# Scores of a differential attention: four products over 128 rows for a component and block of queries, or six over 64 rows

## The chip, the cores and the metric

The kernel runs on one core of one Trainium2 chip. Its time is the device time of one launch in microseconds (us); the kernel before took 3059.82 us (median of 3 runs, 3057.39 to 3063.07). The work is spread over the core's engines, which run side by side and meet at semaphores: TensorE (PE for its products, PEld for the loads of the stationary operand), VectorE (DVE), ScalarE (ACT), GpSimd (POOL), and SyncE (SP), which issues the DMAs.

## The reference, cut to what matters

The program is a two-layer block followed by a second, one-layer block. Each layer of the first block has three branches; the change touches one of them, the differential attention with 4 heads, each with two components of 64 channels, over 1024 positions:

```
def diff_branch(q, k, v, g, ..., pos):
    q = q.reshape(b_, l_, DIFF_HEADS, 2, DIFF_HD).transpose(3, 0, 2, 1, 4)
    k = k.reshape(b_, l_, DIFF_HEADS, 2, DIFF_HD).transpose(3, 0, 2, 1, 4)
    q = rope(q, pos) * (DIFF_HD ** -0.5)
    k = rope(k, pos)
    ...
    def block(qblk):                       # 128 queries at a time
        s = jnp.einsum('cbhqd,cbhkd->cbhqk', qblk, k).astype(jnp.float32)
        p = jax.nn.softmax(s, axis=-1)
        w = p[0] - lam * p[1]
        return jnp.einsum('bhqk,bhkv->bhqv', w.astype(v.dtype), v)
```

So for each of 2 layers, 4 heads and 8 blocks of 128 queries, two score matrices of 128 x 1024 are needed, one for each component, each a product over 64 channels. All data are float32.

## The kernel before, in words

**Products in two parts.** Float32 values that go through the large products are split into a high part H (rounded to the type fp32r) and a low part L = value - H, both of which are stored as fp32r. A product of two such values is taken as H\*H + H\*L + L\*H. `split` does the splitting: a copy on ScalarE (L162) and a subtraction on VectorE (L163).

**Preparing a head.** `diff_prep` projects queries and keys of one head (128 channels, two components of 64), 512 positions at a time, applies the rotary embedding (`raw`, a copy `xs` with channel groups swapped by four DMAs, two products on GpSimd, a sum on VectorE) and then stacks: for component 0 the tile `q0` holds H in its rows 0 to 63 and L in rows 64 to 127, for component 1 `q1` holds L above and H below; the same for `k0` and `k1`. That takes two half-height copies on ScalarE (L773, L774) and two half-height subtractions on VectorE (L775, L776) for each 512 positions. For the keys, two more tiles `ksw` are made by four DMAs (L781, L782), with the halves of `k0` and `k1` swapped. All are tiles of the tag "in" (10 buffers in common with other work); `raw` and `xs` share the two buffers of the tag "pr".

**Scores.** `diff_attend` then needs, for a component and 512 keys, two products over all 128 rows: stack times stack (L797: H\*H + L\*L) and stack times swapped stack (L798: H\*L + L\*H). For a block of 128 queries that makes 2 components x 2 halves of the keys x 2 = 8 products with 512 columns. A component's 1024 scores lie in a PSUM tile `psc` of the tag "big", of which there are two. VectorE takes the negative maximum (L800), ScalarE the exponential with its sum (L803), which also ends the use of the `psc` tile. The weights are combined on VectorE and GpSimd, transposed on TensorE (`pt`, L822), copied (`wT`, L823), and multiplied with the values (`pav`, L827).

**What sets the order.** The program is written as generators: while a head's blocks run, a `Filler` puts projections of later heads (`pj`, L234) between them, so many microseconds' worth per step (RATE); for the last head the output projection (`output`, `pout`, L724) takes that place. A scheduler orders the instructions of each engine from that: at each point it takes, of those whose operands and buffers it reckons to be ready, the one of highest priority. Each engine then works through its list strictly in order, and waits at semaphores. `Burst` is a helper of other stages of the kernel (L388, L411, L452): its first product has the priority of its place, and all later ones of the burst have a much higher one and are tied behind the first. It does not ask that they all be ready when the first is. Products there use part of the rows of the array: `psl` (L411) has 32 or 64 rows to a product, each row group writing a PSUM bank of its own.

The stages that matter here: attention of layer 1 runs from about 432 to 822 us (heads 0 to 3 start at about 432, 540, 638 and 709 us), of layer 2 from about 1281 to 1667 us (1281, 1397, 1484, 1555). From 754 and 1600 us on the output projection runs beside the last head.

Of the kernel before, what the change touches and what calls it, by code (L numbers as in the profile page):

```python
# [9 lines left out]
F32 = mybir.dt.float32  # L10
F32R = mybir.dt.float32r
U8 = mybir.dt.uint8
AF = mybir.ActivationFunctionType
ALU = mybir.AluOpType
# [4 lines left out]
P = 128  # L19
T = 1024  # L20
# [138 lines left out]
def split(k, raw, H, L, leng=None):  # L159

    nc = k.nc
    nc.scalar.copy(H, raw)  # L162
    (leng or nc.vector).tensor_tensor(L, raw, H.bitcast(F32), ALU.subtract)  # L163
# [88 lines left out]
def proj_cm(k, W, c0, m, half):  # L252

    ps = k.pj.tile([P, 512], F32, tag="pj", name="pj")
    terms = []
    for kt in range(KT):
        wh, wl = W.part(kt)
        hh, hl = k.hH[half][:, kt, :], k.hL[half][:, kt, :]
        terms += [(x[:, c0:c0 + m], y) for x, y in ((wh, hh), (wh, hl), (wl, hh))]
    yield from accumulate(k, ps[:m, :], terms)  # L260
    return ps
# [16 lines left out]
def rstd_of(k, ssq, n, scale, pool, tag):  # L278

    nc = k.nc  # L280
    r = pool.tile([P, n], F32, tag=tag, name=tag)
    nc.gpsimd.tensor_scalar(r, ssq, scale, EPS, ALU.mult, ALU.add)  # L282
    nc.gpsimd.tensor_tensor(r, r, k.mhalf[:, :n], ALU.pow)  # L283
    return r
# [216 lines left out]
def layer(k, l, xin, xout):  # L501
# [110 lines left out]
    for pair in range(2):  # L612
        F.add(f"d{2 * pair}", diff_prep(k, 2 * pair, w_in))
        F.add(f"dv{pair}", values(1824 + pair * 256, ("at", "v")[pair]))
        F.add(f"dg{pair}", gates(2336 + pair * 256, slice(128, 256)))
        F.add(f"d{2 * pair + 1}", diff_prep(k, 2 * pair + 1, w_in))
# [39 lines left out]
    for hd in range(4):  # L656
        stk = F.need(f"d{hd}")
        v, sg = F.need(f"dv{hd // 2}"), F.need(f"dg{hd // 2}")
        att = diff_attend(k, l, hd, stk, v, (hd % 2) * P, sg)
        if hd < 3:  # L660
            run(beside(att, mods), RATE["diff"][hd])
            continue
        for _ in mods:
            pass
        if l == DEPTH - 1:
            for _ in context_norm(k):
                pass
        F.drain()
        out = output(k, l, xin, xout)
        next(out)  # L670
        for i, _ in enumerate(att):
            if i > 2 and i % 3 == 2:
                next(out)
        early = context(k) if l == DEPTH - 1 else iter(())
        for _ in out:
            pass
        k.tc.cur_priority -= EARLY
        for _ in early:
            pass
        k.tc.cur_priority += EARLY  # L680
# [71 lines left out]
def diff_prep(k, hd, w_in):  # L752

    nc = k.nc
    Wq = Weights(k, w_in[:, 800 + hd * P:928 + hd * P], P)
    Wk = Weights(k, w_in[:, 1312 + hd * P:1440 + hd * P], P)
    stk = {}
    for nm, W in (("q", Wq), ("k", Wk)):
        s0 = k.wk.tile([P, T], F32R, tag="in", name=nm + "0")
        s1 = k.wk.tile([P, T], F32R, tag="in", name=nm + "1")  # L760
        for half in range(2):
            hs = slice(half * 512, half * 512 + 512)
            ps = yield from proj_cm(k, W, 0, P, half)
            raw = k.wk.tile([P, 512], F32, tag="pr", name="raw")
            xs = k.wk.tile([P, 512], F32, tag="pr", name="xs")
            nc.scalar.activation(raw, ps, AF.Copy, scale=0.125 if nm == "q" else 1.0)  # L766
            for g in range(4):
                g2 = g ^ 1
                nc.sync.dma_start(xs[g * 32:g * 32 + 32, :], raw[g2 * 32:g2 * 32 + 32, :])
            nc.gpsimd.tensor_tensor(raw, raw, k.rcos[:, hs], ALU.mult)  # L770
            nc.gpsimd.tensor_tensor(xs, xs, k.rsin[:, hs], ALU.mult)
            nc.vector.tensor_tensor(raw, raw, xs, ALU.add)
            nc.scalar.copy(s0[0:64, hs], raw[0:64, :])  # L773
            nc.scalar.copy(s1[64:128, hs], raw[64:128, :])  # L774
            nc.vector.tensor_tensor(s0[64:128, hs], raw[0:64, :], s0[0:64, hs].bitcast(F32), ALU.subtract)  # L775
            nc.vector.tensor_tensor(s1[0:64, hs], raw[64:128, :], s1[64:128, hs].bitcast(F32), ALU.subtract)  # L776
        stk[nm] = (s0, s1)
    sw = []
    for c in range(2):
        s = k.wk.tile([P, T], F32R, tag="in", name="ksw")  # L780
        nc.sync.dma_start(s[0:64, :].bitcast(F32), stk["k"][c][64:128, :].bitcast(F32))  # L781
        nc.sync.dma_start(s[64:128, :].bitcast(F32), stk["k"][c][0:64, :].bitcast(F32))  # L782
        sw.append(s)
    return stk["q"], stk["k"], sw


def diff_attend(k, l, hd, stks, v, vc0, sg):
    nc = k.nc
    sq_, sk, sw = stks
    for qt in range(NT):  # L790
        qs = slice(qt * P, qt * P + P)
        ps_, Z = [], []
        for c in range(2):
            ps = k.big.tile([P, T], F32, tag="big", name="psc")
            for kh in range(2):
                ks = slice(kh * 512, kh * 512 + 512)
                nc.tensor.matmul(ps[:, ks], sq_[c][:, qs], sk[c][:, ks], start=True, stop=False)  # L797
                k.mark = nc.tensor.matmul(ps[:, ks], sq_[c][:, qs], sw[c][:, ks], start=False, stop=True)  # L798
            nm = k.st.tile([P, 1], F32, tag="nm", name="nm")
            nc.vector.tensor_reduce(nm, ps, axis=AX.X, op=ALU.max, negate=True)  # L800
            p = k.wk.tile([P, T], F32, tag="U" if c and qt % 2 and hd < 3 else "be", name="p")
            z = k.st.tile([P, 1], F32, tag="Z", name="Z")
            nc.scalar.activation(p, ps, AF.Exp, bias=nm, accum_out=z)  # L803
            ps_.append(p)
            Z.append(z)
        rz = k.st.tile([P, 2], F32, tag="rz", name="rz")
        nc.vector.reciprocal(rz[:, 0:1], Z[0])
        nc.vector.reciprocal(rz[:, 1:2], Z[1])
        sc = k.st.tile([P, 1], F32, tag="sc", name="sc")
        nc.vector.scalar_tensor_tensor(sc, Z[0], rz[:, 1:2], k.nlam[:, l:l + 1], ALU.mult, ALU.mult)  # L810
        yield
        w = ps_[0]
        a, b = slice(0, W_CUT), slice(W_CUT, T)
        nc.vector.scalar_tensor_tensor(w[:, a], ps_[1][:, a], sc, ps_[0][:, a], ALU.mult, ALU.add)
        nc.gpsimd.tensor_scalar_mul(ps_[1][:, b], ps_[1][:, b], sc)  # L815
        nc.gpsimd.tensor_tensor(w[:, b], ps_[1][:, b], ps_[0][:, b], ALU.add)
        wT = k.wk.tile([P, KT, P], F32, tag="at", name="wT")
        for g in range(2):
            pt = k.sm.tile([P, 512], F32, tag="sm", name="pt")
            for j in range(4):  # L820
                c = g * 4 + j
                k.mark = nc.tensor.transpose(pt[:, j * P:(j + 1) * P], w[:, c * P:(c + 1) * P], k.ident)  # L822
            nc.scalar.copy(wT[:, g * 4:g * 4 + 4, :], pt.rearrange("p (j t) -> p j t", j=4))  # L823
        yield
        po = k.sm.tile([P, 512], F32, tag="sm", name="pav")
        for kt in range(KT):
            k.mark = nc.tensor.matmul(po[:, :P], wT[:, kt, :], v[kt][:, vc0:vc0 + P], start=kt == 0, stop=kt == KT - 1)  # L827
        sq = k.st.tile([P, 256], F32, tag="sq", name="sq", bufs=1)
        ss = k.st.tile([P, 1], F32, tag="ss", name="ss")
        nc.scalar.activation(sq[:, :P], po[:, :P], AF.Square, scale=rz[:, 0:1], accum_out=ss)  # L830
        r = rstd_of(k, ss, 1, 1.0 / P, k.st, "rs")
        rr = k.st.tile([P, 1], F32, tag="rr", name="rr")
        nc.vector.tensor_tensor(rr, r, rz[:, 0:1], ALU.mult)
        y = k.wk.tile([P, 256], F32, tag="y", name="y")
        nc.vector.scalar_tensor_tensor(y[:, :P], po[:, :P], rr, sg[qt][:, vc0:vc0 + P], ALU.mult, ALU.mult)
        nc.sync.dma_start(k.ydram[qt][:, 256 + hd * P:384 + hd * P], y[:, :P])
        yield
# [585 lines left out]
HEADS = (slice(0, 64), slice(64, 128))  # L1423
# [635 lines left out]
```

## Time and profile before

| what | before |
|---|---|
| median of 3 runs | 3059.82 us |
| the profiled execution, its own time | 3056.68 us |
| span of its instructions | 3054.9 us |
| TensorE products busy | 2770.3 us (91%) |
| VectorE busy | 1881.9 us (62%) |
| ScalarE busy | 1251.4 us (41%) |
| GpSimd busy | 1010.8 us (33%) |
| mean granted clock of TensorE | 0.962 of full |

The profiled execution took 1.8 us more than its span; that stretch lies outside the instructions. Busy time of TensorE is made of modelled ends: a product of 512 columns is shown as 0.40 us long, while the next starts 0.23 us after it. What a product costs the engine is therefore read from the starts of neighbours (called the pitch below), and not from the durations.

### The profile page before, as it was taken

To read this page: it belongs to the slowest core of one execution; us is meant where nothing else is said; L and a number is where in the kernel's file an instruction comes from. 1 tells how busy PE (TensorE), PEld (TensorE's weight loads), DVE (VectorE), ACT (ScalarE), POOL (GpSimd) and SP (SyncE) were. 2 spreads that over 40 slices of the span, in tenths; PEclk is the share of its full clock that TensorE was granted. 3 is DMA by queue.
4 is the path that set the end of the run, shared out by engine and by line. 5 is a ranking of instruction groups with operands and counts; after the bars stand their busy time and mean duration, and the time that the engine had idled before them with its cause. 6 is when DMAs were issued, how large, how long until landed. Compare 5 with 4: busy or idle time off the path is not lost. (4 is left out here: it accounts for less than half of the span.)

```text
span 3054.9 us, 56014 instructions
## 1 busy us (share of the span) xinstructions
PE 2770.3 (91%) x21790; PEld 2344.4 (77%) x21790; DVE 1881.9 (62%) x3777; ACT 1251.4 (41%) x2791; POOL 1010.8 (33%) x1124
## 2 busy tenths in 40 slices
PE   7899889897989998899979899998888999989999
PEld 4788677885768887788958778886776677769889
DVE  4668686566445686866564456576777664346661
ACT  4222145655434212355554443434353433345520
POOL 1224447754202243476452123321332120010042
PEclk9899899998999998999989999998999999999999
DMA  3111122324331101223243535352445361254463
GB/s 112 29 44 36 39 66 77 90 54 132 114 140 32 43 29 38 67 83 93 69 126 120 172 92 144 108 143 75 110 124 129 94 167 47 61 161 134 152 205 97
DMA packets 353346, 294.02 MB, mean 96 GB/s; under 512 B 145174, under 2 KB 302742, under 8 KB 353080
## 3 DMA queue, kind: packets, MB, share of 16 engines
q1 hardware_dynamic: 353080, 290.43, 32.7%
q8 instruction: 172, 2.82, 0.4%
q14 instruction: 94, 0.77, 0.1%
HBM read 198.79 MB, written 74.78 MB: 90 GB/s over the span
## 5 line engine op out<-in xcount | busy, mean ns | idle before, releaser
L163 DVE TENSOR_TENSOR wL<-wr,wH 128x512 fp32r<-128x512 f32 (+1 forms) x259 | 200.0, 776 | 244.8 <-ACT wH L162 235.3
L234 PE MATMUL pj<-wH,hH 128*128 128x256 f32 x1024 | 295.3, 290 | 16.7 <-ACT wH L162 10.7
L234 PE MATMUL pj<-wL,hH 128*128 128x256 f32 x1024 | 292.8, 286 | 2.4 <-DVE wL L163 2.4
L234 PE MATMUL pj<-wH,hL 128*128 128x256 f32 x1024 | 291.8, 285 | 0.0
L162 ACT CAST wH<-wr 128x512 fp32r<-128x512 f32 (+1 forms) x259 | 159.1, 617 | 297.3 <-PE pj L234 181.2
L234 PE MATMUL pj<-H,wH 128*128 128x512 f32 (+1 forms) x592 | 242.4, 412 | 5.6 <-DVE naz L1608 4.1
L234 PE MATMUL pj<-H,wL 128*128 128x512 f32 (+1 forms) x592 | 243.6, 412 | 0.0
L234 PE MATMUL pj<-L,wH 128*128 128x512 f32 (+1 forms) x592 | 242.7, 410 | 0.0
L234 PE MATMUL pj<-hH,wH 128*128 128x512 f32 (+1 forms) x544 | 222.6, 410 | 11.9 <-ACT raw L766 7.3
L234 PE MATMUL pj<-hL,wH 128*128 128x512 f32 (+1 forms) x544 | 223.2, 410 | 0.0
L234 PE MATMUL pj<-hH,wL 128*128 128x512 f32 (+1 forms) x544 | 222.6, 409 | 0.6 <-DVE wL L163 0.6
L234 PEld LDWEIGHTS pj<-wH,hH 128*128 128x128 f32 x1024 | 194.8, 191 | 24.2 <-ACT wH L162 12.0
L282 POOL TENSOR_SCALAR rs<-ss 128x1 f32<-128x1 f32 (+2 forms) x190 | 62.9, 331 | 442.1 <-DVE ss L730 135.2
L234 PEld LDWEIGHTS pj<-wL,hH 128*128 128x128 f32 x1024 | 195.3, 191 | 6.5 <-DVE wL L163 3.7
L234 PEld LDWEIGHTS pj<-wH,hL 128*128 128x128 f32 x1024 | 195.2, 191 | 2.3
L800 DVE TENSOR_REDUCE nm<-psc 128x1 f32<-128x1024 f32 x128 | 155.0, 1217 | 35.2 <-PE psc L798 34.9
L803 ACT ACTIVATE p<-psc,nm 128x1024 f32<-128x1024 f32 x128 | 142.9, 1117 | 75.5 <-DVE nm L800 45.4
L827 PE MATMUL pav<-v,wT 128*128 128x128 f32 x1024 | 138.4, 286 | 17.7 <-ACT wT L823 15.7
L827 PEld LDWEIGHTS pav<-v,wT 128*128 128x128 f32 x1024 | 130.2, 200 | 30.8 <-ACT wT L823 24.9
L283 POOL TENSOR_TENSOR rs<-rs,mhalf 128x1 f32<-128x1 f32 (+2 forms) x190 | 148.0, 782 | 11.6
L815 POOL TENSOR_SCALAR p<-p,sc 128x320 f32<-128x320 f32 x64 | 102.6, 1603 | 126.3 <-DVE sc L810 92.7
L234 PEld LDWEIGHTS pj<-H,wH 128*128 128x128 f32 (+1 forms) x592 | 112.1, 189 | 31.9 <-DVE naz L1608 4.5
(426 smaller groups left out, 7692.5 us busy)
## 6 DMA issues: line engine op xcount, KB each, us to landing
wr<-in_w_in_dram SPq DMA_DIRECT2D x240, 256.0 KB
modw<-in_mod_w_dram SPq DMA_DIRECT2D x48, 256.0 KB
xs<-raw SPq DMA_DIRECT2D x128, 64.0 KB
ksw<-k SPq DMA_DIRECT2D x32, 256.0 KB
wor<-in_w_out_dram SPq DMA_DIRECT2D x16, 512.0 KB
yt<-y SPq DMA_DIRECT2D x16, 512.0 KB
xh<-xh SPq DMA_DIRECT2D x32, 256.0 KB
gd<-gth SPq DMA_DIRECT2D x32, 256.0 KB
```

The costliest lines, as they stand in the source:

```text
L162: nc.scalar.copy(H, raw)
L163: (leng or nc.vector).tensor_tensor(L, raw, H.bitcast(F32), ALU.subtract)
L234: mm = k.nc.tensor.matmul(ps, x, y, start=i == 0, stop=i == len(terms) - 1)
L282: nc.gpsimd.tensor_scalar(r, ssq, scale, EPS, ALU.mult, ALU.add)
L283: nc.gpsimd.tensor_tensor(r, r, k.mhalf[:, :n], ALU.pow)
L800: nc.vector.tensor_reduce(nm, ps, axis=AX.X, op=ALU.max, negate=True)
L803: nc.scalar.activation(p, ps, AF.Exp, bias=nm, accum_out=z)
L815: nc.gpsimd.tensor_scalar_mul(ps_[1][:, b], ps_[1][:, b], sc)
L827: k.mark = nc.tensor.matmul(po[:, :P], wT[:, kt, :], v[kt][:, vc0:vc0 + P], start=kt == 0, stop=kt == KT - 1)
```

## The change

Queries and keys are now split as whole tiles of 128 rows: `H` and `L` of `q`, `H` and `L` of `k`, with component 0 in rows 0 to 63 and component 1 in rows 64 to 127, by one `split` for each 512 positions. The swapped tiles and their DMAs are gone. For a block of queries, both `psc` tiles are taken first, and twelve products in a `Burst` follow: for each half of the keys and each of H\*H, H\*L and L\*H, one product over rows 0 to 63 (component 0) and one over rows 64 to 127 (component 1), in turn. L\*L is no longer computed. `HEADS` are these two row slices.

```diff
--- before.py
+++ after.py
@@ -756,8 +756,8 @@
     Wk = Weights(k, w_in[:, 1312 + hd * P:1440 + hd * P], P)
     stk = {}
     for nm, W in (("q", Wq), ("k", Wk)):
-        s0 = k.wk.tile([P, T], F32R, tag="in", name=nm + "0")
-        s1 = k.wk.tile([P, T], F32R, tag="in", name=nm + "1")
+        H = k.wk.tile([P, T], F32R, tag="in", name=nm + "H")
+        L = k.wk.tile([P, T], F32R, tag="in", name=nm + "L")
         for half in range(2):
             hs = slice(half * 512, half * 512 + 512)
             ps = yield from proj_cm(k, W, 0, P, half)
@@ -770,32 +770,25 @@
             nc.gpsimd.tensor_tensor(raw, raw, k.rcos[:, hs], ALU.mult)
             nc.gpsimd.tensor_tensor(xs, xs, k.rsin[:, hs], ALU.mult)
             nc.vector.tensor_tensor(raw, raw, xs, ALU.add)
-            nc.scalar.copy(s0[0:64, hs], raw[0:64, :])
-            nc.scalar.copy(s1[64:128, hs], raw[64:128, :])
-            nc.vector.tensor_tensor(s0[64:128, hs], raw[0:64, :], s0[0:64, hs].bitcast(F32), ALU.subtract)
-            nc.vector.tensor_tensor(s1[0:64, hs], raw[64:128, :], s1[64:128, hs].bitcast(F32), ALU.subtract)
-        stk[nm] = (s0, s1)
-    sw = []
-    for c in range(2):
-        s = k.wk.tile([P, T], F32R, tag="in", name="ksw")
-        nc.sync.dma_start(s[0:64, :].bitcast(F32), stk["k"][c][64:128, :].bitcast(F32))
-        nc.sync.dma_start(s[64:128, :].bitcast(F32), stk["k"][c][0:64, :].bitcast(F32))
-        sw.append(s)
-    return stk["q"], stk["k"], sw
+            split(k, raw, H[:, hs], L[:, hs])
+        stk[nm] = (H, L)
+    return stk["q"], stk["k"]
 
 
 def diff_attend(k, l, hd, stks, v, vc0, sg):
     nc = k.nc
-    sq_, sk, sw = stks
+    (qH, qL), (kH, kL) = stks
     for qt in range(NT):
         qs = slice(qt * P, qt * P + P)
         ps_, Z = [], []
-        for c in range(2):
-            ps = k.big.tile([P, T], F32, tag="big", name="psc")
+        pss = [k.big.tile([P, T], F32, tag="big", name="psc") for _ in range(2)]
+        with Burst(k) as burst:
             for kh in range(2):
                 ks = slice(kh * 512, kh * 512 + 512)
-                nc.tensor.matmul(ps[:, ks], sq_[c][:, qs], sk[c][:, ks], start=True, stop=False)
-                k.mark = nc.tensor.matmul(ps[:, ks], sq_[c][:, qs], sw[c][:, ks], start=False, stop=True)
+                for i, (x, y) in enumerate(((qH, kH), (qH, kL), (qL, kH))):
+                    for c, r in enumerate(HEADS):
+                        burst(nc.tensor.matmul(pss[c][:, ks], x[r, qs], y[r, ks], start=i == 0, stop=i == 2))
+        for c, ps in enumerate(pss):
             nm = k.st.tile([P, 1], F32, tag="nm", name="nm")
             nc.vector.tensor_reduce(nm, ps, axis=AX.X, op=ALU.max, negate=True)
             p = k.wk.tile([P, T], F32, tag="U" if c and qt % 2 and hd < 3 else "be", name="p")
```

The scheduler's list for TensorE shows where the products stand. `k0`, `q0`, `k1`, `q1` and `ksw` are the old tiles, `kH`, `kL`, `qH` and `qL` the new ones; two numbers behind `psc` are the two components of one block of queries. Before, at the first block of head 0 in layer 1:

```order
L234 MATMUL pj_3940<-wH_3924,hH_184 128x256 [waits Activation_49]
L797 MATMUL psc_4464<-k0_3345,q0_3082 128x512
L798 MATMUL psc_4464<-ksw_3532,q0_3082 128x512
L797 MATMUL psc_4474<-k1_3346,q1_3083 128x512
L234 MATMUL pj_3940<-wL_3925,hH_184 128x256 [waits DVE_49]
L234 MATMUL pj_3940<-wH_3924,hL_186 128x256
L234 MATMUL pj_3940<-wH_3924,hH_184 128x256
L234 MATMUL pj_3940<-wL_3925,hH_184 128x256
L234 MATMUL pj_3940<-wH_3924,hL_186 128x256
L798 MATMUL psc_4474<-ksw_3535,q1_3083 128x512 [waits DMAHW1_49,DMAHW0_49]
L797 MATMUL psc_4474<-k1_3346,q1_3083 128x512
```

After, at the same block:

```order
L234 MATMUL pj_3926<-wH_3904,hH_184 128x256 [waits Activation_49]
L790 MATMUL psc_4450<-kH_3341,qH_3082 128x512
L790 MATMUL psc_4451<-kH_3341,qH_3082 128x512
L790 MATMUL psc_4450<-kL_3342,qH_3082 128x512
L790 MATMUL psc_4451<-kL_3342,qH_3082 128x512
L790 MATMUL psc_4450<-kH_3341,qL_3083 128x512
L790 MATMUL psc_4451<-kH_3341,qL_3083 128x512
L790 MATMUL psc_4450<-kH_3341,qH_3082 128x512
L790 MATMUL psc_4451<-kH_3341,qH_3082 128x512
```

Here the two components stand in turn, twelve products in one piece, and the projection `pj` that stood between the parts of the second component has moved behind them. Before, at the second block of head 2 in layer 1, the first component (its second component stands some 25 rows later, behind other products):

```order
L234 MATMUL pj_6309<-wH_5807,hL_187 128x256
L797 MATMUL psc_6778<-k0_5111,q0_4925 128x512 [waits Activation_49]
L798 MATMUL psc_6778<-ksw_5293,q0_4925 128x512
L797 MATMUL psc_6778<-k0_5111,q0_4925 128x512
L798 MATMUL psc_6778<-ksw_5293,q0_4925 128x512
L822 MATMUL pt_6554<-ident_60,p_6518 128x128 [waits Activation_49]
L822 MATMUL pt_6554<-ident_60,p_6518 128x128 [waits Pool_49]
```

After, at the same block:

```order
L234 MATMUL pj_6391<-wH_5789,hL_187 128x256
L790 MATMUL psc_6800<-kH_5099,qH_4909 128x512 [waits Activation_49]
L790 MATMUL psc_6800<-kL_5100,qH_4909 128x512
L790 MATMUL psc_6800<-kH_5099,qL_4910 128x512
L790 MATMUL psc_6800<-kH_5099,qH_4909 128x512
L790 MATMUL psc_6800<-kL_5100,qH_4909 128x512
L790 MATMUL psc_6800<-kH_5099,qL_4910 128x512
L820 MATMUL pav_6599<-v_3725,wT_6565 128x128 [waits Activation_49]
L820 MATMUL pav_6599<-v_3725,wT_6565 128x128 x3
L815 MATMUL pt_6664<-ident_60,p_6639 128x128 [waits PE_49]
L790 MATMUL psc_6801<-kH_5099,qH_4909 128x512 [waits Activation_49]
L790 MATMUL psc_6801<-kL_5100,qH_4909 128x512
```

Here the six products of one component stand in a row, all over the same 64 rows, then other products over 128 rows, and then the six of the other component, which have a wait of their own for ScalarE. Counted over all 64 blocks (2 layers x 4 heads x 8), the new list has the 768 products in 93 unbroken groups; 163 pairs of them stand in turn as written (326 products), and 442 products stand behind one of the same component or of another block. By layer and head:

| layer, head | pairs | products alone | groups |
|---|---|---|---|
| 1, 0 | 36 | 24 | 10 |
| 1, 1 | 32 | 32 | 9 |
| 1, 2 | 6 | 84 | 15 |
| 1, 3 | 2 | 92 | 14 |
| 2, 0 | 36 | 24 | 10 |
| 2, 1 | 30 | 36 | 11 |
| 2, 2 | 13 | 70 | 13 |
| 2, 3 | 8 | 80 | 11 |

The other stages that use parts of the rows (L388, L411, L452) keep their number of groups.

## Rows read from the trace of the kernel before

**Rows 1.** The page's first part: busy us, share of the span and instructions by engine.

```profile
PE 2770.3 (91%) x21790; PEld 2344.4 (77%) x21790; DVE 1881.9 (62%) x3777; ACT 1251.4 (41%) x2791; POOL 1010.8 (33%) x1124
```

**Rows 2.** Busy time by stretch of the differential attention, both layers.

```profile
core 0: us, PE busy (x) PEld busy (x) DVE busy (x) ACT busy (x) POOL busy (x), PEclk, DMA share, GB/s
432.00:540.00 108.00, 100.41 (x618) 86.89 (x618) 76.31 (x133) 63.90 (x142) 78.24 (x78) 1.00 0.32 88
...
638.00:709.00 71.00, 67.41 (x416) 58.02 (x415) 47.31 (x82) 41.53 (x87) 40.97 (x43) 1.00 0.22 56
709.00:754.00 45.00, 29.52 (x137) 23.45 (x136) 30.46 (x53) 24.52 (x50) 17.75 (x20) 0.78 0.55 156
...
1484.00:1555.00 71.00, 67.08 (x413) 57.72 (x412) 46.91 (x80) 41.10 (x84) 39.79 (x40) 1.00 0.21 54
1555.00:1600.00 45.00, 26.96 (x136) 21.83 (x135) 30.81 (x55) 25.43 (x54) 25.38 (x30) 0.81 0.57 173
...
sum 776.00, PE 703.00 PEld 606.58 DVE 488.46 ACT 437.13 POOL 429.94; mean PE 70.30 PEld 60.66 DVE 48.85 ACT 43.71 POOL 42.99
```

**Rows 3.** Waits of TensorE, 432 to 822 us: us in all, times, longest.

```profile
PE pj L234 <- ACT raw L766: 8.0, 5, 3.4
PE pt L822 <- DVE y L835: 8.0, 4, 5.2
...
PE psc L798 <- DMA ksw<-k: 3.2, 1, 3.2
```

**Rows 4.** The same, 1281 to 1667 us.

```profile
PE psc L797 <- ACT p L803: 10.6, 9, 3.2
...
PE pj L234 <- ACT raw L766: 2.9, 3, 1.8
...
PE psc L798 <- DMA ksw<-k: 0.6, 1, 0.6
```

**Rows 5.** Groups of the score products: shapes, count | busy us, mean ns | idle before.

```profile
L797 PE MATMUL psc<-k,q 128*128 128x512 f32 x256 | 109.1, 427 | 16.2 <-ACT p L803 16.2
...
L798 PE MATMUL psc<-ksw,q 128*128 128x512 f32 x256 | 104.4, 408 | 3.7 <-DMA ksw<-k 3.7
```

**Rows 6.** TensorE in order of time in head 2: start us, us long, what.

```profile
658.52 0.40 PE L797 MATMUL psc<-k,q 128*128 128x512 f32 x1
658.75 0.39 PE L798 MATMUL psc<-ksw,q 128*128 128x512 f32 x1
658.98 0.39 PE L797 MATMUL psc<-k,q 128*128 128x512 f32 x1
```

**Rows 7.** TensorE in order of time around a burst of 64-row products.

```profile
1140.13 0.28 PE L234 MATMUL pj<-wL,hH 128*128 128x256 f32 x1
1140.35 1.16 PE L411 MATMUL psl<-Qt,Kt 64*128 64x128 f32 x16
1141.44 0.39 PE L234 MATMUL pj<-wH,hL 128*128 128x256 f32 x1
1141.66 0.28 PE L234 MATMUL pj<-wH,hH 128*128 128x256 f32 x1
1141.78 0.28 PE L234 MATMUL pj<-wL,hH 128*128 128x256 f32 x1
```

**Rows 8.** TensorE in order of time around a burst of 32-row products.

```profile
119.21 1.17 PE L411 MATMUL psl<-Qt,Kt 32*128 32x128 f32 x32
120.32 0.38 PE L234 MATMUL pj<-wH,hH 128*128 128x256 f32 x1
```

**Rows 9.** Stacking the keys: ns min/median/max, first and last start, forms.

```profile
L773 ACT CAST k<-raw x16: 602/618/621, 402.1 to 1557.9; 64x512 fp32r<-64x512 f32 x16
...
L775 DVE TENSOR_TENSOR k<-raw,k x16: 684/794/1523, 405.1 to 1559.4; 64x512 fp32r<-64x512 f32 x16
```

**Rows 10.** TensorE in order of time in head 3, at the second swapped tile.

```profile
726.37 0.50 PE L798 MATMUL psc<-ksw,q 128*128 128x512 f32 x1 [3.15 <-DMA ksw<-k]
```

## The prediction

> **What bounds the kernel now.** I read the page first: TensorE is busy 91% of the span, the next engine 62% [rows 1]. That is an average, so the stretches of the differential attention come next [rows 2]. The reader is to see that in head 2 TensorE is busy 67.4 of 71 us in layer 1 and 67.1 of 71 in layer 2, with VectorE and ScalarE at two thirds or less: there every product that is added in its list pushes the rest back. The opening of head 3 is another matter (709 to 754 and 1555 to 1600 us): TensorE is busy 29.5 and 27.0 of 45 us, at a mean granted clock of 0.78 and 0.81, so part of these stretches runs at the lower of the two levels, 1.2 GHz; a chain of other work sets the pace. Over all ten stretches TensorE is idle 776.0 - 703.0 = 73.0 us. The waits say for what: for `raw`, which frees the PSUM buffer of a projection, 8.0 + 2.9 us; for `ksw`, 3.2 + 0.6 us; the rest for steps of the softmax [rows 3, 4].
>
> **The score products.** Before, there are 512, all over 128 rows [rows 5]. Busy time misleads, since ends are modelled; the starts of neighbours stand 0.23 us apart (658.52, 658.75, 658.98) [rows 6]; that pitch is what a product costs. 512 x 0.23 = 117.8 us of TensorE.
>
> After, there are 768 over 64 rows. What a pair costs is not in the trace for 512 columns, so I take it from narrower ones. A burst of 16 products over 64 rows, two row groups in turn, starts at 1140.35 and lasts 1.16 us; a burst of 32 over 32 rows, four row groups in turn, lasts 1.17 [rows 7, 8]. Eight rounds either way: with four products to a round the time is that of two, so row groups in turn run side by side. For a pair of 512 columns the bounds are thus 0.23 (side by side) and 0.46 (one after the other); I take 0.23, the case that the rows show. Two products behind one another over the same row group don't share anything: they cost 0.23 each, as products over 128 rows do, for the columns are the same 512.
>
> Such a burst also costs something at its edges. From the last `pj` ahead of it (1140.13) to the second behind it (1141.66) are 1.53 us; two `pj` pitches of 0.12 (1141.66 to 1141.78) and eight rounds of 0.11 leave 1.53 - 0.23 - 0.89 = 0.40 us [rows 7]. It lies at the front, where the array empties and the first weights are loaded with nothing beside them, and again at the back (1141.44 to 1141.66 is 0.22 where 0.12 is usual). The other burst is as long from its start to the next `pj`, 1.11 us against 1.09 [rows 7, 8]. Bounds for the edges of a burst of 512-column products: 0, if wide products hide them, and 0.40; I take 0.40, since emptying and a first load don't depend on the columns that follow.
>
> Now the list of TensorE. Written as pairs, all 64 blocks would need 6 x 0.23 + 0.40 = 1.78 us against 8 x 0.23 = 1.84: little is to be had, 4 us in all. But the list has only 163 pairs; 442 products stand alone and there are 93 groups. The reason is visible in its waits: the two `psc` buffers come free one after the other, each at the end of an exponential; the first product of the burst needs only component 0, it is placed as soon as that buffer is reckoned free, and the five others of component 0, with the highest priority of all, follow at once while component 1 is not ready. A block split so costs 12 x 0.23 + 2 x 0.40 = 3.56 us, 1.72 more than before. The sum: (163 + 442) x 0.23 + 93 x 0.40 = 139.2 + 37.2 = 176.4 us, less 117.8: **+58.6 us** of TensorE, of which by the table of pairs and groups heads 0 and 1 bring 14.6 and heads 2 and 3 bring 44.0. A burst that stays whole must also wait for both exponentials, with TensorE's whole list behind it; a wait for one costs 1.2 us today (10.6 us in 9) [rows 4]. Since such a burst stays whole only where both buffers are reckoned free, I take 0; the most is one such wait for each of the 25 whole blocks, 30 us.
>
> **What it removes.** For each 512 positions of q or k two ScalarE copies of 0.62 us become one over 128 rows, and two VectorE subtractions of 0.69 (the lesser ends; one median is 0.79) become one [rows 9]. These engines are not the bound, so this counts only where TensorE waits for `raw`: `raw` and `xs` share two buffers, so the next `raw` waits until the last subtraction has read the old one, and that chain is 1.3 us shorter. TensorE waits for it 5 + 3 times, 10.9 us; 8 x 1.3 = 10.4 is the most, 0 the least; I take -7. The `ksw` DMAs (8 MB over the program) go with their waits, 3.8 us on TensorE, the longest at 726.37 [rows 10]; where such a wait goes, the softmax of the same blocks is next and not far behind. I take -4 (0 to -8, as VectorE too starts earlier there).
>
> **What is covered.** In the two openings of head 3 there is idle TensorE time, 15.5 and 18.0 us [rows 2]; three to four split blocks fall in each, 6 us a layer. These added products also lie on the chain of their blocks, so I let half be covered, -6 (0 to -12). Of the other 73.0 - 33.5 = 39.5 us of idle time some waits are for a step that started after a score product and are not shortened; I let -5 (0 to -12) go. If the cover is gone, both terms are zero.
>
> Sum: 58.6 - 7 - 4 - 6 - 5 = **+37 us**. On the profiled execution, 3056.7 + 37 = 3094; that one lies 3.1 us under the median of the runs, so for the median I forecast 3097. Its own range: with nothing gained and nothing covered 3118; with edges half as large and every gain at its most 58.6 - 18.6 - 10.4 - 8 - 12 - 12 = -2, so 3058. Neither end is likely with all its terms together; I keep 3070 to 3122.
>
> **A rule weighed.** In the trace, weight loads run behind products over the same rows: `pj` products of 256 columns stand 0.12 apart although each brings its own load, and a load with nothing beside it showed as 0.10 more (0.22 against 0.12) [rows 7]. In the Trainium skill, "TensorE: Matmul & The Clock Gate", section "Part 3: Packing small matmuls", a load overlaps products in flight only when its row group differs. Here the trace disagrees for full height, and in the burst too, where in each round of 0.11 both row groups take a new load; by the rule the products that stand alone would each pay for theirs.
>
> **Rivals.** (a) The waits take it: the idle 73.0 us swallow the added 58.6, and the removed waits show. Place: all heads; price: all covered, 10.9 + 3.8 gained, 3045. It decides when more than 44 of the 58.6 fall into idle time. Against it: head 2 alone gains 12.0 and 9.6 us of products where TensorE is idle 3.6 and 3.9. (b) No gain and no loss: the edges cost nothing with wide products (-37) and the cover is as I have it: 58.6 - 37.2 - 22 = -1, 3059. For it: no burst of 512 columns is in the trace. Against: the 0.40 is the same for 16 and 32 products. (c) The pairs don't run side by side at 512 columns, the change doesn't do what it says: 163 x 0.23 = +37 more, so 3134. Against it: the two bursts [rows 7, 8]. (d) Loads over the same row group are not hidden: 442 x 0.10 = +44 more, so 3141; the trace speaks against it, as said.
>
> **How the numbers follow.** Forecast 0.80; (a) 0.07, (b) 0.05, (c) 0.05, (d) 0.03. A difference of 0.2%, 6 us, is about what a measurement here can tell from none. Faster comes from (a): 0.07. Within 0.2% comes from (b) and 0.01 of the forecast's lower tail: 0.06. Slower is the rest of the forecast with (c) and (d): 0.87. The range for 8 in 10: the forecast's own, 3070 to 3122, holds nearly all of its 0.80; stretched to 3066 below and 3124 above.
>
> **What would show it.** In the profile after, a pair of `psc` products should start within 0.01 us of each other and the next pair 0.23 later; products alone should stand 0.23 apart; each group should lose about 0.4 us at its edges. Head 2 should be longer by about 10 us in each layer, heads 0 and 1 by a few us together, the opening of head 3 by little or nothing; the waits for `ksw` must be gone, and those for `raw` less. VectorE and ScalarE should lose some 22 and 20 us of busy time. I am wrong if head 2 keeps its length, if a group shows no edges, or if the time that heads 0 and 1 gain by a shorter preparation outweighs their 14.6.

## The result and the profile after

| | before | after |
|---|---|---|
| median, 4 runs each | 3058.67 us (3057.39 to 3063.07) | 3105.43 us (3096.87 to 3107.78) |
| profiled execution, own time | 3056.7 us | 3105.35 us |
| its span | 3054.9 us | 3103.6 us |
| TensorE busy in it | 2770.3 us | 2828.8 us |

The ratio is 1.0145, with a 95% interval of 1.0123 to 1.0167: the change makes the kernel slower by 47 us. The forecast was 3097 us, range 3066 to 3124.

The page's first part of the kernel after, the line that answers to [rows 1]:

```profile
PE 2828.8 (91%) x22046; PEld 2370.6 (76%) x22046; DVE 1841.1 (59%) x3745; ACT 1230.3 (40%) x2759; POOL 1003.6 (32%) x1124
```

TensorE has 58.5 us more, in 256 more products; VectorE has 40.8 less and ScalarE 21.1 less.

Next, TensorE of the kernel after in order of time (start us, us long, what), first around a group that stayed whole, then around a block that was split. An "x2" row is two products at practically the same start, one of each component:

```profile
489.86 0.40 PE L234 MATMUL pj<-hH,wL 128*128 128x512 f32 x1
490.18 0.50 PE L790 MATMUL psc<-kH,qH 64*128 64x512 f32 x2
490.52 0.39 PE L790 MATMUL psc<-kL,qH 64*128 64x512 f32 x2
490.75 0.40 PE L790 MATMUL psc<-kH,qL 64*128 64x512 f32 x2
490.99 0.39 PE L790 MATMUL psc<-kH,qH 64*128 64x512 f32 x2
491.22 0.40 PE L790 MATMUL psc<-kL,qH 64*128 64x512 f32 x2
491.45 0.40 PE L790 MATMUL psc<-kH,qL 64*128 64x512 f32 x2
491.78 0.66 PE L815 MATMUL pt<-ident,p 128*128 128x128 f32 x4
...
654.68 0.49 PE L790 MATMUL psc<-kH,qH 64*128 64x512 f32 x1
655.02 0.39 PE L790 MATMUL psc<-kL,qH 64*128 64x512 f32 x1
655.25 0.39 PE L790 MATMUL psc<-kH,qL 64*128 64x512 f32 x1
655.48 0.39 PE L790 MATMUL psc<-kH,qH 64*128 64x512 f32 x1
655.71 0.39 PE L790 MATMUL psc<-kL,qH 64*128 64x512 f32 x1
655.93 0.39 PE L790 MATMUL psc<-kH,qL 64*128 64x512 f32 x1
656.25 1.16 PE L820 MATMUL pav<-v,wT 128*128 128x128 f32 x8
```

Read the distances of the starts. Six pairs take 1.27 us from the first start to the last and 1.60 to the next TensorE work; six products alone take 1.25 and 1.57. So a pair costs what one product costs, and a product alone does half the work in the same time. The usual distance is 0.23. The excess stands at the edges: 0.32 instead of 0.23 ahead of the first group (489.86 to 490.18), 0.34 to its second pair, 0.33 behind its last. A fourth piece follows behind the first product over 128 rows after a group, as in [rows 7], where 0.22 stood in place of 0.12. Four pieces of about 0.1 make the 0.40 of the forecast.

The waits of TensorE after, for the two stretches of [rows 3] and [rows 4], 400 to 870 us and 1281 to 1720 us (us in all, times, longest):

```profile
PE psc L790 <- ACT p L796: 11.1, 5, 5.4
PE pav L820 <- DVE y L828: 6.0, 3, 2.7
PE pt L815 <- DVE y L828: 5.0, 3, 3.7
...
PE pj L234 <- ACT raw L766: 0.4, 1, 0.4
```

```profile
PE pav L820 <- DVE y L828: 8.7, 6, 2.5
PE psc L790 <- ACT p L796: 7.4, 2, 5.4
```

The waits for `ksw` are gone, and 10.9 us for `raw` have become 0.4. In their place TensorE waits longer for the softmax step `y`: 26.2 us in all in both layers (`pav`, `pt` and `tps`), 17.2 before.

Where the 48.7 us of span came from is seen by cutting the program at work that both kernels have: the first score product of each layer, the first product of layer 2 (`tps<-ident,hn`) and the first one of the second block of the program (`tps<-ident,hx`), which the change does not touch. That gives, in order, the attention of layer 1 with what runs beside it, the stretch between (the other branches of layer 2), and the attention of layer 2. Before, and then after (columns as in [rows 2]):

```profile
432.00:884.80 452.80, 409.39 (x2444) 350.84 (x2444) 269.57 (x458) 248.52 (x553) 232.51 (x256) 0.97 0.32 99
884.80:1281.50 396.70, 363.71 (x3042) 307.92 (x3043) 272.87 (x439) 114.77 (x211) 131.69 (x150) 0.95 0.16 46
1281.50:1718.60 437.10, 395.38 (x2372) 340.15 (x2372) 262.44 (x456) 233.12 (x505) 217.14 (x246) 0.97 0.35 104
```

```profile
429.80:895.80 466.00, 433.17 (x2572) 361.05 (x2572) 261.04 (x446) 240.26 (x541) 227.94 (x256) 0.97 0.28 89
895.80:1296.70 400.90, 367.88 (x3041) 311.66 (x3042) 266.12 (x435) 111.98 (x207) 132.13 (x150) 0.94 0.15 43
1296.70:1753.30 456.60, 418.35 (x2501) 348.17 (x2501) 250.97 (x444) 225.15 (x493) 215.65 (x246) 0.97 0.30 93
```

The two attention stretches, which hold the change, are 32.7 us longer (13.2 and 19.5): TensorE is busy 46.8 more, and its idle time falls from 85.1 to 71.1, by 14.0. The stretch between them is 4.2 us longer with the same products. The start of the differential attention comes 2.2 earlier, so the first block ends 34.7 later. The other 14.0 us lie in the second block (1336.3 us before, 1350.3 after), at the same number of products. So 18.2 of the 48.7 us lie where nothing was edited. The scheduler has put the instructions of the second block into another order: of its 8187 products in TensorE's list, 6576 stand at the same place as before. The clock differs as well: by the clock record of the trace, TensorE stood at the lower level, 1.2 GHz, for 99.0 us of the second block before and for 114.8 after. It is busy 6.1 us longer there; the other 7.9 us are idle time. Whether the change is to blame for this is a question for the experiments.

### The profile page after: what moved, and what is told of

Its sections match the earlier page's. It is cut to its first block, busy times and chain, and to the rows that moved or that the text cites. A ratio compares the mean times of both kernels' runs of the same rounds, so it can differ in the third digit from the quotient of the medians.

```text
span 3103.6 us, 56381 instructions
## 1 busy us (share of the span) xinstructions
PE 2828.8 (91%) x22046; PEld 2370.6 (76%) x22046; DVE 1841.1 (59%) x3745; ACT 1230.3 (40%) x2759; POOL 1003.6 (32%) x1124
## 5 line engine op out<-in xcount | busy, mean ns | idle before, releaser
L234 PE MATMUL pj<-wH,hH 128*128 128x256 f32 x1024 | 297.8, 292 | 18.2 <-ACT wH L162 15.4
L820 PE MATMUL pav<-v,wT 128*128 128x128 f32 x1024 | 143.9, 291 | 26.4 <-DVE y L828 14.7
L808 POOL TENSOR_SCALAR p<-p,sc 128x320 f32<-128x320 f32 x64 | 108.5, 1695 | 130.8 <-DVE sc L803 82.5
L283 POOL TENSOR_TENSOR rs<-rs,mhalf 128x1 f32<-128x1 f32 (+2 forms) x190 | 143.3, 756 | 11.3
```

The source lines that it names most:

```text
L234: mm = k.nc.tensor.matmul(ps, x, y, start=i == 0, stop=i == len(terms) - 1)
```

## The experiments

Seven kernels were run. In the edits that follow, "whole" is the kernel after with one thing changed, and three others are built on it. All medians of a table row come from the same chip as the run of before beside them.

| kernel | median us | before beside it | ratio, 95% interval | attention, both layers | stretch between | second block |
|---|---|---|---|---|---|---|
| after | 3105.43 | 3058.67 | 1.0145 (1.0123 to 1.0167) | +32.7 | +4.2 | +14.0 |
| whole | 3047.43 | 3059.63 | 0.9958 (0.9943 to 0.9973) | +10.0 | -8.5 | -7.4 |
| whole_halves | 3064.39 | 3059.63 | 1.0009 (0.9996 to 1.0022) | +35.5 | -19.7 | -6.5 |
| whole_cmajor | 3079.84 | 3059.63 | 1.0062 (1.0038 to 1.0086) | +30.7 | -0.2 | -3.4 |
| whole_two | 3091.39 | 3059.63 | 1.0104 (1.0077 to 1.0131) | +29.4 | +0.1 | +3.9 |
| before_share | 3074.84 | 3067.00 | 1.0028 (1.0015 to 1.0040) | +5.7 | +1.4 | +18.6 |
| after_share | 3099.95 | 3067.00 | 1.0106 (1.0085 to 1.0127) | +38.0 | +3.6 | +6.4 |
| alone | 3176.79 | 3067.00 | 1.0342 (1.0300 to 1.0384) | +116.1 | +0.1 | +12.1 |

The last three columns are stretches of one profiled execution each, in us against the profile of before (889.9, 396.7 and 1336.3). In whole_halves some 170 products of the stretch between stand in the attention of layer 2, so there only the sum of the two is to be compared. before_share has the list of before up to the second block, and its first two stretches are 7.1 us longer all the same: that is how much such a stretch moves from one execution to another.

### Keeping the bursts whole

The first product of each burst is made to depend on both exponentials of the block before, so that the scheduler places it only where both `psc` buffers are reckoned free. Its list then has 384 pairs, no product alone, and 64 groups.

```
+ mm = nc.tensor.matmul(pss[c][:, ks], x[r, qs], y[r, ks], ...)
+ if burst.first is None:
+     for e in k.exps:   # the exponentials of the block before
+         info = DependencyInfo(DependencyClass.Sync, DependencyReason.DATA)
+         k.tc.add_manual_dep(mm.ins, e.ins.name, info, reason="both buffers are free")
+     k.exps = []
+ burst(mm)
...
+ k.exps.append(nc.scalar.activation(p, ps, AF.Exp, bias=nm, accum_out=z))
```

> The changed kernel, with one edit: the first product of a block's burst also depends on both exponentials of the block before, so that the list has all 64 blocks whole (384 pairs, none alone, 64 groups; the changed kernel has 163 pairs, 442 alone, 93 groups). Theory A (products that stand alone, and edges of groups, cost the time): TensorE has 384 x 0.23 + 64 x 0.40 = 113.9 us of score products against 176.4 in the changed kernel and 117.8 before; 62 us less than in the changed kernel, of which 50 to 62 should reach the time, so 3043 to 3056, and the version is level with the kernel before or some us faster, since the waits for raw and ksw stay away. Rival B (the burst's wait for both buffers, with TensorE's list behind it, costs the time): now every block has that wait, so it is no faster than the changed kernel, 3105 or more.

Measured: 3047.43 us, ratio 0.9958 (0.9943 to 0.9973). That is 58 us below the kernel after, and the fastest of all that ran. The same three stretches of whole:

```profile
431.30:891.20 459.90, 409.78 (x2572) 346.09 (x2572) 259.96 (x446) 238.91 (x540) 226.88 (x256) 0.95 0.29 90
891.20:1279.40 388.20, 358.76 (x3043) 304.27 (x3043) 266.81 (x435) 111.86 (x208) 128.03 (x150) 0.97 0.15 45
1279.40:1719.40 440.00, 393.90 (x2501) 333.01 (x2501) 248.51 (x444) 223.63 (x492) 216.14 (x246) 0.96 0.32 97
```

In the attention TensorE is busy 47.8 us less than after (by the forecast's prices 62.5: 176.4 less 64 x 1.78) and 1.1 less than before. So the added work of TensorE did not come from 64-row products as such; it came with the way in which the list splits them. But TensorE is idle 25.1 us more than after, 96.2 instead of 71.1, and so the attention gets only 22.7 us shorter. That the whole kernel gains 58, as theory A had it, is in part luck: 12.7 us of the 55.3 between the two profiles lie in the stretch between and 21.4 in the second block, where nothing was edited.

The waits that grew are behind the softmax, not in front of the score products. From layer 2 of whole (1270 to 1710 us):

```profile
PE pav L826 <- ACT wT L822: 20.5, 14, 3.4
PE pav L826 <- DVE y L834: 8.3, 6, 2.3
PE psc L790 <- ACT p L802: 6.5, 4, 3.3
```

After had 5.9 us there for the row `pav <- wT`. One reading is that component 0's scores of a block start later when they wait for component 1's buffer, so that its transposes and `wT` come later. Another is that a TensorE with less work comes to the same softmax steps sooner and waits there. No run parts the two. TensorE also stood at 1.2 GHz for longer in the attention: 81.9 us by the clock record, against 61.4 after and 51.2 before.

Whole beats before by 12 us, but its profile does not place this gain in the changed part: its attention is 10.0 us longer than before's, and the stretch between and the second block are 8.5 and 7.4 us shorter. So whether the edit itself gains anything over before is not shown.

### Going back to copies and subtractions by halves

Whole again, with the stacking as two copies and two subtractions over 64 rows where `split` has one of each over 128:

```
- split(k, raw, H[:, hs], L[:, hs])
+ for r in HEADS:
+     nc.scalar.copy(H[r, hs], raw[r, :])
+ for r in HEADS:
+     nc.vector.tensor_tensor(L[r, hs], raw[r, :], H[r, hs].bitcast(F32), ALU.subtract)
```

> The kernel with whole bursts, and the removed preparation put back in part: the four half-height copies and subtractions for each 512 positions in place of two of full height (the swapped tiles stay away). The list has 383 pairs and 2 products alone. Theory A': the shorter chain behind raw was worth about 7 us, so this is 0 to 10 us slower than with whole bursts, and waits of TensorE for raw appear again (10.9 us in the kernel before). Rival: these engines are never what TensorE waits for, and the time is the same within 3 us.

Measured: 3064.39 us, 17 more than whole, and more than was expected of the preparation. VectorE is busy 26.0 us more and ScalarE 21.4, as many as the extra instructions make. The time did not go where it was looked for: TensorE's waits for `raw` are 1.4 us in all. Layer 2 of whole_halves (1270 to 1710 us):

```profile
PE pt L824 <- DVE y L837: 13.3, 4, 8.3
PE pav L829 <- ACT wT L825: 11.7, 12, 3.0
PE pt L824 <- ACT wT L825: 7.7, 3, 5.4
```

In whole `pt` waits 3.5 us for `y` and 0.6 for `wT` there, but `pav` waits longer for `wT`, 20.5. Over the three stretches of the first block TensorE is idle 144.2 us where whole has 125.6, 18.6 more, and busy 4.3 less; that is the 14.3 by which these stretches are longer. So the shorter preparation may be worth more than was thought, through the softmax: VectorE and ScalarE would get to it earlier. That is argued and not shown: the two lists are not the same (383 pairs and 2 products alone here, and the 170 products that stand in another stretch), and part of the 17 us, or all of it, may be that.

### One component after the other, in one burst

Whole again, with all six products of component 0 ahead of the six of component 1:

```
- for kh ...: for i, (x, y) ...: for c, r in enumerate(HEADS):
+ for c, r in enumerate(HEADS): for kh ...: for i, (x, y) ...:
```

> The kernel with whole bursts, but the twelve products of a block in the order component 0, then component 1, not in turn: one group a block, same products, same wait. Theory A: a block costs 11 x 0.23 + 0.40 = 2.93 us against 1.78 (the last of the one component and the first of the other make one pair), 73.6 us more of TensorE; 60 to 74 in the time over the kernel with whole bursts, so 3105 to 3130. Rival C (row groups in turn do not run side by side at 512 columns, the order within a group is of no weight): the same time as with whole bursts within 5 us.

Measured: 3079.84 us, 32 more than whole; between the profiles it is 30, of which 20.7 lie in the attention and 8.3 in the stretch between. Neither side had this number. TensorE of whole_cmajor in order of time, one group:

```profile
436.41 0.49 PE L790 MATMUL psc<-kH,qH 64*128 64x512 f32 x1
436.74 0.39 PE L790 MATMUL psc<-kL,qH 64*128 64x512 f32 x1
436.97 0.39 PE L790 MATMUL psc<-kH,qL 64*128 64x512 f32 x1
436.98 0.61 PE L790 MATMUL psc<-kH,qH 64*128 64x512 f32 x2
437.31 0.51 PE L790 MATMUL psc<-kL,qH 64*128 64x512 f32 x2
437.55 0.51 PE L790 MATMUL psc<-kH,qL 64*128 64x512 f32 x2
437.78 0.39 PE L790 MATMUL psc<-kH,qH 64*128 64x512 f32 x1
438.01 0.39 PE L790 MATMUL psc<-kL,qH 64*128 64x512 f32 x1
438.24 0.39 PE L790 MATMUL psc<-kH,qL 64*128 64x512 f32 x1
438.56 0.49 PE L471 MATMUL po<-bd,f 128*128 128x128 f32 x2
```

Twelve products alone would take 12 rounds, 11 x 0.23 = 2.5 us from the first start to the last. They take 1.83. Component 0 runs at its 0.23: 436.41, 436.74, 436.97, then the second of the two starts in the row at 436.98 (436.978 and 437.207). Component 1 begins at 436.978, while three products of component 0 that stand ahead of it in the list have not started; from there the two run beside one another. (The rows do not name the component; it is read from the spacing, 0.23 us within each series.) So order does count, but a product over the other rows starts up to three places early: eight rounds instead of six, and 0.34 in place of 0.23 once more where component 1 begins. From the first start to the next TensorE work such a block takes 2.16 us where a block of whole takes 1.59 (medians of all blocks at full clock), 64 x 0.57 = 36.5 us in all; the time of the attention shows 0.57 of it. The Trainium skill, "TensorE: Matmul & The Clock Gate", section "Part 3: Packing small matmuls", holds that matmuls start and end strictly in their order; for the starts of two row groups this trace shows otherwise.

The overlap doesn't reach over most split blocks: there the products of component 1 come after others over 128 rows (`pav` at 656.25 above). But ten of the 163 pairs of the kernel after are only the seams of such runs of one component behind the other, so some of its 442 products alone have a partner after all.

### Twice the edges

Whole again, with one product over 128 rows and 512 columns between the two halves of the keys; its scores are overwritten, so it adds a product and one more group, with its edges, to each block:

```
  for kh in range(2):
      ks = slice(kh * 512, kh * 512 + 512)
+     if kh:
+         burst(nc.tensor.matmul(pss[0][:, ks], qH[:, qs], kH[:, ks], start=True, stop=True))
```

> The kernel with whole bursts, with one product over 128 rows and 512 columns put between the two halves of the keys in each burst (its scores are overwritten by the next products): 64 products and 64 more changes from part of the rows to all and back. Theory A (edges cost 0.40 us): 64 x (0.23 + 0.40) = 40 us more of TensorE, 32 to 40 in the time over the kernel with whole bursts. Rival D (edges are hidden by wide products): 64 x 0.23 = 15 us, 12 to 15 in the time.

Measured: 3091.39 us, 44 more than whole. By the forecast's prices it adds 64 x (0.23 + 0.40) = 40.3 us; without edges, 14.7. Here the time alone does not decide: between the profiles it is 38 us, of which the attention has 19.4, closer to rival D's 12 to 15 than to the 32 to 40 of theory A, while 8.6 lie in the stretch between and 11.3 in the second block. The rows decide. TensorE of whole_two in order of time:

```profile
491.30 0.50 PE L792 MATMUL psc<-kH,qH 64*128 64x512 f32 x2
491.64 0.40 PE L792 MATMUL psc<-kL,qH 64*128 64x512 f32 x2
491.87 0.39 PE L792 MATMUL psc<-kH,qL 64*128 64x512 f32 x2
492.19 0.49 PE L789 MATMUL psc<-kH,qH 128*128 128x512 f32 x1
492.62 0.51 PE L792 MATMUL psc<-kH,qH 64*128 64x512 f32 x2
492.96 0.40 PE L792 MATMUL psc<-kL,qH 64*128 64x512 f32 x2
```

From the last pair of one half (491.87) to the first of the next (492.62) are 0.75 us, and 0.34 instead of 0.23 follow: with the product's own round, 0.75 + 0.34 - 3 x 0.23 = 0.40. The edge is a cost of its own and does not hide behind 512 columns.

### Another list for the block that the change leaves alone

The second block was 14 us longer after the change. Either it carries something on from the first block, or its list just came out worse. One planner cost of that block, F_SHARE for "ctx", was raised from 2.88 to 2.98, in before and in after. In before this leaves the first block's list as it was, and in the second 3938 of 8187 products stay at their place.

```
- "ctx": 2.88
+ "ctx": 2.98
```

> The kernel before, with one number of the second block's filler changed (F_SHARE ctx from 2.88 to 2.98): the list of the first block stays as it is to the last product, the list of the second block holds the same 8187 products with only 3938 at the same place. Theory S (the second block's time hangs on how its list falls out): the first block, up to the first transposes of hx at 1719 us, keeps its time within 3 us, and the second block's 1336 us move by 5 to 15 us with no change of work. Rival: a list with the same work takes the same time within 3 us.

> The changed kernel with the same number changed: same list of the first block, 3961 of 8187 products of the second at the same place. In the changed kernel the second block took 14 us more than before, though nothing of it was edited. Theory S (that is how its list fell out): the first block is 34 us longer than in the kernel before with that number, as it was, and the second block is no longer the same 14 us longer than there, but anything from 10 us less to 10 us more. Rival E (the change reaches into the second block by itself, through what it hands over): again 12 to 16 us longer than in the kernel before with that number.

Measured: before_share 3074.84 us, ratio 1.0028 (1.0015 to 1.0040); after_share 3099.95, ratio 1.0106 (1.0085 to 1.0127). The second block as one stretch, of before, before_share, after and after_share in turn:

```profile
1718.60:3054.90 1336.30, 1231.71 (x10895) 1033.06 (x10893) 792.64 (x1954) 529.95 (x1295) 290.12 (x300) 0.96 0.43 122
```

```profile
1725.40:3080.30 1354.90, 1240.03 (x10895) 1033.12 (x10893) 790.42 (x1954) 531.79 (x1295) 296.86 (x300) 0.96 0.43 120
```

```profile
1753.30:3103.60 1350.30, 1237.80 (x10895) 1036.72 (x10893) 785.61 (x1954) 530.29 (x1295) 287.00 (x300) 0.96 0.42 121
```

```profile
1757.10:3099.80 1342.70, 1235.76 (x10895) 1031.76 (x10893) 790.54 (x1954) 531.35 (x1295) 288.96 (x300) 0.96 0.43 121
```

With the old cost the change goes with +14.0 us here, with the other one with -12.2, a little past the 10 us less that theory S allowed. A delay carried on from the first block would have the same sign in both. The attention, in contrast, is longer by 32.7 and by 32.3 (38.0 - 5.7). So the price of the change proper is some 32 to 33 us, and the whole difference was 47 us with one list of the untouched block and 25 (3099.95 - 3074.84) with another.

One caution: before_share's profiled execution took 3082 us, the longest of its ten, and its first block ended 6.8 us later with the same list, where it was expected to keep its time within 3. Its span is 25.4 us above before's, while the medians on one chip differ by 7.8. So the 18.6 us of its second block are not all its list's. By the medians the change costs 25.1 us there, less than the 32.3 of the attention, so the sign holds, but it is nearer -7 than -12. The clock goes along with these times: in the second block TensorE stood at 1.2 GHz for 99.0, 110.5, 114.8 and 105.8 us in the four executions shown.

### As few pairs as the scheduler makes

The kernel after with one component after the other and without a burst. Its list has 37 pairs, 694 products alone and 259 groups:

```
- pss = [k.big.tile(...) for _ in range(2)]
- with Burst(k) as burst: for kh ...: for i ...: for c, r in enumerate(HEADS): ...
+ for c, r in enumerate(HEADS):
+     ps = k.big.tile([P, T], F32, tag="big", name="psc")
+     for kh ...: for i, (x, y) ...:
+         k.mark = nc.tensor.matmul(ps[:, ks], x[r, qs], y[r, ks], start=i == 0, stop=i == 2)
```

> The changed kernel with the products over 64 rows kept, but written component by component and without a burst: 37 pairs, 694 products alone, 259 groups in the list. Theory A (products alone and edges of groups): (37 + 694) x 0.23 + 259 x 0.40 = 272 us of TensorE, 154 more than in the kernel before; in the other kernels 0.6 to 0.75 of what was added reached the time of the first block, so 90 to 120 us, and the whole between 3140 and 3190. Rival (edges hide behind other products, only the products alone count): 168 - 118 = 50 us of TensorE, 30 to 40 in the time, so 3085 to 3105.

Measured: 3176.79 us, 110 more than before on its chip, inside what the theory of split blocks gives. By the prices (37 + 694) x 0.23 + 259 x 0.40 - 117.8 = +154 us of TensorE; in the attention it is busy 156.5 us more and idle 40.4 less, so that the stretches grew by 116.1, 0.75 of the added work. For after that share is 32.7 / 58.6 = 0.56. Not all of the 156.5 is products and edges: TensorE stood at 1.2 GHz for 119.5 us of these stretches, against 51.2 before.

## Why the prediction was right, point by point

**Pitch and pairs** held: 0.23 us for a pair side by side and for a product alone, read off the rows above. Rival (c), pairs one after the other, is out. So is rival (d): six products over the same row group, each with its own load, start 0.23 apart, with nothing added. The rule of the Trainium skill, "TensorE: Matmul & The Clock Gate", section "Part 3: Packing small matmuls", that a load overlaps only products of another row group, is not borne out by these six either.

**The edges**, taken at 0.40 between bounds of 0 and 0.40, held: 0.40 in whole_two's rows, and four pieces of 0.1 in the rows of after. Rival (b) is out.

**The split of the list** is the cause of the added TensorE work, as the prediction put it: taken away alone, in whole, it takes all of it along (46.8 us of busy time in the attention came with the change, 47.8 went in whole). Of the 32.7 us by which the attention grew, 22.7 went; the rest came back as idle time. The size was off. The added work was put at +58.6 us, and the page's +58.5 only looks like a hit: 6.1 of it lie in the second block, 4.2 in the stretch between and 1.4 ahead of the attention, where the work is the same. In the attention it is 46.8. The term that was mis-sized is the one of before, 512 x 0.23 = 117.8: start to start, with idle time taken off, its 512 products took 134.0 us, since 22 of them ran at the lower clock and others lost some 0.1 to 0.2 us beside a wait. Those of after took 161.0, and some 19 more for the two pieces of each edge that fall on their neighbours, 180 against the forecast's 176.4.

**The removed preparation**, -7 with a bound of -10.4: the waits for `raw` fell by 10.5 us [rows 3, 4], to the bound. **The `ksw` waits**, -4: all 3.8 went. Together 14.3, and TensorE's idle time in the attention fell by 14.0.

**The cover**, -6 and -5, is the term that failed. If the idle time had swallowed 11 us of the added products, it would have fallen by some 25; it fell by no more than the removed waits. Some idle time did go, 5.7 us that TensorE waited for `bd`, a step of another stage beside the attention, but longer waits for the softmax made up for it: 17.2 us for `y` became 26.2, and 16.1 for an exponential 18.5. So, in the attention: 46.8 - 14.0 = +32.7 (by the unrounded sums), against 58.6 - 22 = +37. Two sizes were off, by 11.8 and by 8 us, in opposite directions, and that the sum comes so close is luck.

**A whole burst waits for both exponentials**, taken at 0 with 30 at most: right for after, where such waits rose by 2.4 us. In whole, where all 64 blocks are held together, idle time is 25.1 us more than after and 11.1 more than before; how much of that is the wait for both is open.

**Heads.** Here the prediction was wrong. Head 2 was to be 10 us longer in each layer, heads 0 and 1 a few together. From first score product to first score product, the heads grew thus:

| | head 0 | head 1 | head 2 | head 3 with the tail |
|---|---|---|---|---|
| layer 1 | 108.5 to 126.6 | 97.7 to 91.8 | 71.3 to 75.7 | 175.3 to 171.9 |
| layer 2 | 115.9 to 129.7 | 86.5 to 85.5 | 71.5 to 73.1 | 163.3 to 168.3 |

Much of this comes from the work between the blocks, which is no fixed part of a head. By the counts of the trace, head 0 of layer 1 holds 16 `pj` of 256 columns, 24 of 512, 16 `pav` and 12 `pt` more after than before: at 0.23 for 512 columns and about 0.12 for the others some 11 of its 18.1 us. Head 1 holds 24 and 8 `pj` and 8 `pt` fewer, head 2 16 `pav`, 8 `pj` and 4 `pt` fewer, 3.4 us. The forecast set the added products of a head beside the old contents of its window; the new contents stood in the new order, and were not counted. Head 2 of layer 2 grew by only 1.6 us, which is close to the forecast's own sign of being wrong, that head 2 keeps its length.

**The engines.** ScalarE lost 21.1 us where 20 were forecast. VectorE lost 40.8 where 22 were; 29.3 of this are the preparation's (64 subtractions of half height took 52.7 us, the 32 of full height 23.4), and the rest lies in instructions that the change leaves alone.

**The second block** was no term of the sum. It is why the profiled execution is 3105.35 us and not near 3094, and the experiment on its list says that it need not have had this sign. Rival (a), that the waits take it all, is out: idle time fell, but by 14 us and not by enough.

## What to carry to other kernels

Products over half the rows pay only in pairs, and a pair is made by the list, not by the code that writes the two side by side (in whole_cmajor a partner three places away was still found): count pairs, products alone and groups in the scheduler's order before believing a gain, at one pitch for each round and an edge for each group. If a burst needs two buffers, tie its first product to both, and see whether the waits behind it grow. And where a scheduler orders the whole program, part of a measured difference can lie in stretches that the change leaves alone, so compare stretch by stretch before pricing an edit by the total: of the 55 us between the profiles of after and whole, 34 lay where nothing was edited.

## What the runs showed of the hardware that was not expected

- A product over one row group starts ahead of products over the other row group that stand before it in the list: three places early at 436.98 us in whole_cmajor, 12 products in eight rounds of 0.23 us.
- The edge of a group is four pieces of about 0.1 us, two of them at the change to 64 rows and two at the change back, and 512 columns don't hide them (0.40 us in whole_two, as for 128 columns in [rows 7]).
- The same work of the second block took 1336.3 to 1354.9 us in the four executions shown, with no instruction added or removed in it, and 99.0 to 114.8 us of it at the lower clock. How much of the 18.6 us is the list and how much one execution is open; by medians before_share is 7.8 us longer than before.
